# Deferred vector operations, a one-engine state chain, earlier bias loads and an unsplit modulation in a hybrid decoder step

## Chip, cores and metric

The kernel runs on one NeuronCore of a Trainium2 chip. The metric is the device time of one execution in microseconds (us); before the change it is 2248.98 us, the median of three runs (2247.84 to 2250.97). Engines are called as in the profile: PE (matrix multiply; PEld is its weight load), DVE (vector), ACT (scalar, with the activation functions), POOL (GpSimd) and SP, which issues the DMAs. All five run their own instructions in program order and wait for each other on semaphores.

## The reference

One layer of a conditioned decoder, for a prompt of 2048 tokens and eight sampled sequences of four tokens, model width 1024. The part of the reference that matters:

```
mod = silu(c) @ w_ada + b_ada                       # c: 1 + 8 rows of 1024; w_ada 1024 x 3072
shift, scale, gate = split(mod, 3)
h = rms(x, norm_g) * (1 + scale) + shift
proj = h @ w_in + b_in                              # 1024 x 7176, split into nine parts
y_h = head_rms(hgrn2(q, log f, v), hgrn_norm_g) * silu(hz)              # 8 heads of 128
y_m = (head_rms(sigmoid(mo) * mlstm(...), mnorm_g) + skip * xc) * silu(mz)   # 4 heads of 256
out = x + gate * (concat(y_h, y_m) @ w_out);  y = rms(out, final_g)
```

Both recurrences are computed chunk by chunk, with the state carried from chunk to chunk. All arithmetic is fp32.

## The kernel before

**Precision.** A plain fp32 matrix multiply is slow on PE, so the large products are split: an operand is written as a rounded part (type fp32r, made by ACT) and a remainder (made by DVE or POOL), and three products of parts are summed. `split` (line 205) does this for weights.

**Staging.** The prompt is cut in four segments of 512 tokens (`SEG`), a segment in four chunks of 128. First the modulation is computed (`ada_rows`, line 451): sixteen pieces of w_ada of 512 KB each are loaded, split by ACT and by DVE or POOL (line 461), and multiplied with `scs`, the split silu(c), into four PSUM tiles; `ada_shift_scale` (line 471) adds their two halves, transposes them and adds b_ada and 1. Then `x_modulate` (line 400) writes the normalized, modulated input as `hhi` and `hlo`. After that come 48 units per segment (`run_unit`, line 1444), one per 128 or 256 columns of w_in. A narrow unit is 24 matmuls of 512 columns in two steps (`proj_ct`, line 543), a wide one ("v" and "mo") 24 matmuls of 256 columns for each of four chunks (`proj_tok`, line 556). Split weights are written to DRAM in segment 0 and read back in segments 1 to 3. Last comes the output projection (line 1743).

**Order of the work.** The order on every engine is the order in which the program emits it. Next to the unit streams a list `rec` of generators: one per HGRN head (`hgrn`, line 601), one per mLSTM head (`mlstm`, line 1093), one for the convolution (`conv`, line 1008), and some others. After each step of a unit, `pump` (line 576) first issues stores that have come due, and then lets every generator in `rec`, oldest first, emit its next step. A generator that is appended later stands later in the list. Weights run ahead through a ring of four 8 KB slots per partition (`w8`) and a ring of three raw tiles. PSUM is a ring of eight tiles (`ps_tile`, line 123), taken in turn.

**Chains that the change touches.** A sigmoid is three ACT operations (line 94). In `hgrn` the decays are a sigmoid and a logarithm on ACT, then a scan, a copy and a subtraction on DVE (lines 612 to 616) and a scaling on POOL (617); two steps later, two exponentials, and the products `Ep` and `tn` (630, 631), which PE reads three steps on (639). The state chain of a head (lines 669 to 680) goes chunk by chunk: DVE adds (`U`, 677), POOL scales (678). `hgrn_out` scales by the norm (859) and gates (873, 877), and reads PSUM in both. `mlstm_out` (1291) takes the norm of a head by four ACT squares, a logarithm and an exponential, has DVE make `kap` of it (1313) and POOL scale `num` with it (1315); PE transposes `num` three steps later (1324), and DVE finishes the head (1333 to 1338). `head` and `c_split` (1104, 1127) prepare a chunk of the mLSTM. `bd_prep` (1533) builds block-diagonal weights in segment 0. `bias_bc` (1370) loads the bias of a "v" or "mo" unit at its start. `x_next` (1666) loads an input tile of the next segment and scales it at once on POOL.

Of the kernel before, what the change touches and what calls it, by code (L numbers as in the profile page):

```python
# [8 lines left out]
F32 = mybir.dt.float32  # L9
# [8 lines left out]
P = 128  # L18
# [49 lines left out]
def hymba_step(ctx, tc, flag, halved, x_prompt, x_sample, c_prompt, c_sample, state_hgrn, state_C, state_n, state_m,  # L68
# [140 lines left out]
    class Unit:  # L209
# [26 lines left out]
        def split(self, j):  # L236
# [4 lines left out]
            split(self.raw.pop(j), self.hi[:, :, c], self.lo[:, :, c], pool if self.src is w_in else vec)  # L241
# [7 lines left out]

    def C(nm, k):  # L250
        return cols[:, col[nm] + k:col[nm] + k + 1]
# [4 lines left out]
    sct = S2("sct", [P, KD, 1 + NSEQ])  # L256
# [4 lines left out]
    vec.tensor_tensor(sct[:, :, 1:], sgc[:, KD:].rearrange("p (s k) -> p k s", k=KD),  # L261
                      acol[:, 32:96].rearrange("p (s k) -> p k s", k=KD), op=ALU.mult)

    ML = 32 + 1 + NSEQ + 1
    scs = con.tile([P, KD, ML], F32R, name="scs")
    scp = S2("scp", [P, KD, ML])
    vec.memset(scp, 0.0)
    vec.tensor_copy(scs, scp)
    vec.tensor_copy(scs[:, :, :1 + NSEQ], sct)
    vec.tensor_tensor(scs[:, :, 32:33 + NSEQ], sct, scs[:, :, :1 + NSEQ].bitcast(F32), op=ALU.subtract)  # L270
# [172 lines left out]
    NB = 1 + NSEQ  # L443

    def ada_piece(n):
        k, b = divmod(n, 2)
        t = Bt("wada", [P, D]) if n % 2 else raw_tile()
        sync.dma_start(t, w_ada[k * P:k * P + P, b * D:b * D + D])
        return t

    def ada_rows(step):

        acc = [ps_tile("pada") if b % 2 else ps_tile("pada") for b in range(4)]
        raw = {n: ada_piece(n) for n in range(4)}
        for n in range(2 * KD):
            k, b = divmod(n, 2)
            step(n)
            r = raw.pop(n)
            t = ring.tile([P, 2, D], F32R, tag="w8", name="wadas", bufs=4)
            act(t[:, 0], r, AF.Copy)  # L460
            (pool if n % 4 == 3 else vec).tensor_tensor(t[:, 1], r, t[:, 0].bitcast(F32), op=ALU.subtract)
            for g in range(2):
                c = slice(512 * g, 512 * g + 512)
                for y in range(2):
                    pe.matmul(acc[2 * b + g][:ML], scs[:, k], t[:, y, c], start=(k == 0 and y == 0),
                              stop=(k == KD - 1 and y == 1))
            if n + 4 < 2 * KD:
                raw[n + 4] = ada_piece(n + 4)
        return acc

    def ada_shift_scale(acc):
        rows = Bt("arows", [NB, D])
        rows2 = Bt("arows", [NB, D])
        for b in range(4):
            dst = (rows, rows2)[b // 2][:, 512 * (b % 2):512 * (b % 2) + 512]
            act(dst, acc[b][:NB], AF.Copy)
            vec.tensor_tensor(dst, dst, acc[b][32:32 + NB], op=ALU.add)
        for r, dst, one in ((rows, msh, 0.0), (rows2, msc, 1.0)):
            ps = ps_tile("padt")
            for k in range(KD):  # L480
                pe.transpose(ps[:, k * NB:k * NB + NB], r[:, k * P:k * P + P], ident[:NB, :NB])
            v = ps[:, :KD * NB].rearrange("p (k b) -> p k b", k=KD)
            c0 = KD if one else 0
            vec.scalar_tensor_tensor(dst, v, one, acol[:, c0:c0 + KD, None].to_broadcast([P, KD, NB]),
                                     op0=ALU.add, op1=ALU.add)
        vec.tensor_tensor(msc, msc, C8("norm_g")[:, :, None].to_broadcast([P, KD, NB]), op=ALU.mult)
# [87 lines left out]
    stores = deque()  # L574

    def pump(n=1):
        for _ in range(n):
# [6 lines left out]
            for g in list(rec):  # L584
                if next(g, "end") == "end":
                    rec.remove(g)

# [13 lines left out]
    def hgrn(s, h, d):  # L601
# [10 lines left out]
        vec.tensor_tensor_scan(G[:, :W], hmask[:, :W], G[:, :W], 0.0, op0=ALU.mult, op1=ALU.add)  # L612
        g4 = G[:, :SEG].rearrange("p (c u t) -> p c u t", u=2, t=CH // 2)
        mid = small("mid", [P, NCH, 1])
        vec.tensor_copy(mid, g4[:, :, 0, CH // 2 - 1:CH // 2])
        vec.tensor_tensor(g4[:, :, 0], g4[:, :, 0], mid.to_broadcast([P, NCH, CH // 2]), op=ALU.subtract)
        pool.tensor_scalar(tn[:, :W], tn[:, :W], noml[:, h:h + 1], oml[:, h:h + 1], op0=ALU.mult, op1=ALU.add)  # L617
# [11 lines left out]
        vec.tensor_tensor(beta[:, :NCH - 1], sm[:, 0:NCH - 1], sm[:, NCH + 1:2 * NCH], op=ALU.mult)  # L629
        vec.tensor_tensor(Ep[:, :W], hq[:, :W], Ep[:, :W], op=ALU.mult)  # L630
        vec.tensor_tensor(tn[:, :W], tn[:, :W], G[:, :W], op=ALU.mult)
# [37 lines left out]
        for c in range(NCH):  # L669
# [180 lines left out]
    def hgrn_out(s, h, po, ops):  # L850
# [4 lines left out]
        for c in range(NCH):  # L855
# [3 lines left out]
        vec.tensor_tensor(on[:, :SEG].rearrange("p (c v) -> p c v", c=NCH), po.rearrange("p (c v) -> p c v", c=NCH),  # L859
                          f[:, :, None].to_broadcast([P, NCH, CH]), op=ALU.mult)  # L860
# [12 lines left out]
        vec.tensor_tensor(sz[:, :W], sz[:, :W], y[:, :W], op=ALU.mult)  # L873
# [3 lines left out]
        vec.scalar_tensor_tensor(y[:, :SEG], pn, C("hg", h), sz[:, :SEG], op0=ALU.mult, op1=ALU.mult)  # L877
        if smp:
            pn = ps_tile("pn")
            pe.matmul(pn[:, :NSM], onesm, sq)  # L880
            act(sq, pn[:, :NSM], AF.Ln, bias=epsc)
            act(sq, sq, AF.Exp, scale=-0.5)
            vec.scalar_tensor_tensor(ops, ops, C("hg", h), sq, op0=ALU.mult, op1=ALU.mult)
            vec.tensor_tensor(y[:, SEG:], ops, sz[:, SEG:], op=ALU.mult)
        y_store(s, h, y, W)
# [122 lines left out]
    def conv(s, i, j, d):  # L1008
# [28 lines left out]
        vec.tensor_tensor(xc[:, :W], xc[:, :W], e[:, :W], op=ALU.mult)  # L1037
# [55 lines left out]
    def mlstm(s, i, d):  # L1093
# [10 lines left out]
        def head(c):  # L1104
# [6 lines left out]
            vec.tensor_tensor(dm[:, t], ps[:, :CH], dm[:, t], op=ALU.mult)  # L1111
            st = small("st", [P, 2, CH], 2, F32R)
            act(st[:, 0], dm[:, t], AF.Copy)
            vec.tensor_tensor(st[:, 1], dm[:, t], st[:, 0].bitcast(F32), op=ALU.subtract)
            xw = small("xw", [P, 2, 2 * P], 1, F32R)
            wc = zc[:, c, 2, i:i + 1]
            act(xw[:, 0], ps[:, CH:CH + 2 * P], AF.Copy, scale=wc)
            vec.scalar_tensor_tensor(xw[:, 1], ps[:, CH:CH + 2 * P], wc, xw[:, 0].bitcast(F32), op0=ALU.mult,
                                     op1=ALU.subtract)
            if first and c == 0:  # L1120
                return st, xw, None
# [3 lines left out]
            return st, xw, qs  # L1125

        def c_split():
            t = small("Ch", [P, 2, 2, DH + 2], 1, F32R)
            act(t[:, 0], Cc, AF.Copy)
            vec.tensor_tensor(t[:, 1], Cc, t[:, 0].bitcast(F32), op=ALU.subtract)  # L1130
            return t
# [6 lines left out]
        ch = None if first else c_split()  # L1138
        yield
        yield  # L1140
        for c in range(NCH):
            st, xw, qs = cur
# [25 lines left out]
            if c + 1 < NCH:  # L1168
                ch = c_split()
# [121 lines left out]
    def mlstm_out(s, i, d, num, nums):  # L1291
# [7 lines left out]
        for nm, n, nch, og, floor in sets:  # L1299
# [19 lines left out]
        for j in range(2):  # L1319
# [13 lines left out]
            vec.tensor_tensor(szm[:, j, :W], szm[:, j, :W], e[:, :W], op=ALU.mult)  # L1333
# [538 lines left out]
```

## Time and profile before

| | |
|---|---|
| median of three runs | 2248.98 us |
| the profiled execution | 2243.03 us, its span 2241.2 us |
| instructions | 35168 |
| mean granted clock of PE in it | 0.989 of full |
| data moved by DMA | 405.26 MB, 181 GB/s over the span |

The profiled execution is 1.8 us longer than its span, and 5.95 us (0.3%) shorter than the median of the runs. The busy time of PE is not all work at its peak, since the ends of matmuls are modelled; what an engine's idle time was ended by is inferred from semaphores. A plain fp32 matmul leaves two records of PE in the trace, one of a split product leaves one.

### The profile page before, as it was taken

To read this page: it belongs to the slowest core of one execution; us is meant where nothing else is said; L and a number is where in the kernel's file an instruction comes from. 1 tells how busy PE (TensorE), PEld (TensorE's weight loads), DVE (VectorE), ACT (ScalarE), POOL (GpSimd) and SP (SyncE) were. 2 spreads that over 40 slices of the span, in tenths; PEclk is the share of its full clock that TensorE was granted. 3 is DMA by queue.
4 is the path that set the end of the run, shared out by engine and by line. 5 is a ranking of instruction groups with operands and counts; after the bars stand their busy time and mean duration, and the time that the engine had idled before them with its cause. 6 is when DMAs were issued, how large, how long until landed. Compare 5 with 4: busy or idle time off the path is not lost.

```text
span 2241.2 us, 35168 instructions
## 1 busy us (share of the span) xinstructions
PE 2170.0 (97%) x13594; PEld 1915.1 (85%) x13594; DVE 1268.8 (57%) x2664; ACT 979.1 (44%) x2260; POOL 432.0 (19%) x436
## 2 busy tenths in 40 slices
PE   6999999999999999999999999999999998999998
PEld 3888998787899889899988898888899987888885
DVE  7675657566756574566574555655455675423232
ACT  6445554464443354353444454534444535212121
POOL 3424353341112020212010212110101033000000
PEclk8999999999999999999999999999999999999999
DMA  7676766864546465634465555454555566533330
GB/s 257 214 234 219 262 221 205 302 227 155 189 152 228 167 230 193 217 136 158 179 203 202 189 192 180 162 169 163 146 194 161 174 193 173 165 108 96 93 99 27
DMA packets 225318, 405.26 MB, mean 181 GB/s; under 512 B 24843, under 2 KB 168627, under 8 KB 196470
## 3 DMA queue, kind: packets, MB, share of 16 engines
q1 hardware_dynamic: 225142, 402.92, 54.2%
q8 instruction: 109, 1.79, 0.3%
q14 instruction: 67, 0.55, 0.1%
HBM read 298.43 MB, written 104.44 MB: 180 GB/s over the span
## 4 chain that ended last, share of the span: by engine, by line
PE 68%; DVE 4%; ACT 3%; DMA 1%; issue 1%; POOL 1%; SPq 0%; DVEq 0%; ACTq 0%; POOLq 0%
PE pct L549 27%; PE pout L1743 15%; PE ptok L563 11%; PE p L1151 1%; PE pc L1135 1%; PE pv L1064 1%; PE pp L663 1%; PE pa L639 1%; PE pq L1081 1%; PE po L687 1%; PE po L689 1%; PE psx L1108 1%; ACT st L92 1%; PE p L1135 1%; DMA raw<-in_w_out_dram 1%
## 5 line engine op out<-in xcount | busy, mean ns | idle before, releaser
L549 PE MATMUL pct<-hhi,w 128*128 128x512 f32 (+1 forms) x3200 | 852.0, 354 | 1.2 <-DVE S L697 1.2
L549 PEld LDWEIGHTS pct<-hhi,w 128*128 128x128 f32 x3200 | 552.9, 188 | 74.4 <-issue 3.3
L549 PE MATMUL pct<-hlo,w 128*128 128x512 f32 (+1 forms) x1600 | 560.6, 350 | 0.0
L549 PEld LDWEIGHTS pct<-hlo,w 128*128 128x128 f32 x1600 | 301.0, 188 | 39.2
L563 PE MATMUL ptok<-whi,hhi 128*128 128x256 f32 x1024 | 301.4, 294 | 4.4 <-ACT hhi L92 3.3
L563 PE MATMUL ptok<-whi,hlo 128*128 128x256 f32 x1024 | 291.2, 284 | 0.2 <-DVE hlo L426 0.2
L563 PE MATMUL ptok<-wlo,hhi 128*128 128x256 f32 x1024 | 290.9, 284 | 0.0
L1743 PE MATMUL pout<-wh,y 128*128 128x512 f32 (+1 forms) x792 | 247.2, 391 | 3.0 <-ACT wh L92 3.0
L563 PEld LDWEIGHTS ptok<-whi,hhi 128*128 128x128 f32 x1024 | 197.4, 193 | 7.8 <-ACT hhi L92 3.7
L563 PEld LDWEIGHTS ptok<-wlo,hhi 128*128 128x128 f32 x1024 | 197.6, 193 | 2.3 <-issue 2.2
L563 PEld LDWEIGHTS ptok<-whi,hlo 128*128 128x128 f32 x1024 | 197.3, 193 | 0.9 <-DVE hlo L426 0.9
L1743 PEld LDWEIGHTS pout<-wh,y 128*128 128x128 f32 (+1 forms) x792 | 148.2, 187 | 35.8 <-ACT wh L92 3.5
L1743 PE MATMUL pout<-wl,y 128*128 128x512 f32 (+1 forms) x408 | 159.8, 392 | 1.1 <-POOL wl L1780 0.6
L92 ACT ACTIVATE xo<-oo 128x512 f32<-128x512 f32 (+1 forms) x34 | 21.5, 632 | 249.5 <-DVE oo L1831 249.5
L92 ACT ACTIVATE e<-e 128x512 f32<-128x512 f32 (+1 forms) x160 | 102.0, 638 | 58.9 <-DVE e L1034 54.8
L1826 DVE TENSOR_TENSOR oo<-pout,gate 128x512 f32<-128x512 f32 x32 | 22.0, 687 | 186.3 <-PE pout L1743 185.4
L617 POOL TENSOR_SCALAR tn<-tn,noml,oml 128x512 f32<-128x512 f32 (+1 forms) x32 | 52.6, 1643 | 385.5 <-ACT G L92 384.8
L207 POOL TENSOR_TENSOR w<-raw,w 128x1024 fp32r<-128x1024 f32 x40 | 97.2, 2436 | 113.5 <-ACT w L92 95.1
L121 POOL TENSOR_SCALAR num<-num,fin 128x256 f32<-128x256 f32 x64 | 35.1, 566 | 401.7 <-DVE fin L1313 357.8
L1161 DVE SCALAR_TENSOR_TENSOR Cc<-Cc,dec,pc 128x258 f32<-128x258 f32 x120 | 52.4, 478 | 84.0 <-PE pc L1135 84.0
L1743 PEld LDWEIGHTS pout<-wl,y 128*128 128x128 f32 (+1 forms) x408 | 75.6, 185 | 19.7 <-POOL wl L1780 1.3
L1032 DVE SCALAR_TENSOR_TENSOR xc<-mu,cols,xc 128x512 f32<-128x512 f32 (+1 forms) x120 | 83.7, 698 | 4.2
(403 smaller groups left out, 3792.2 us busy)
## 6 DMA issues: line engine op xcount, KB each, us to landing
w<-wdr SPq DMA_DIRECT2D x120, 1024.0 KB
wdr<-w SPq DMA_DIRECT2D x40, 1024.0 KB
raw<-in_w_in_dram SPq DMA_DIRECT2D x56, 512.0 KB
whi<-wdr SPq DMA_DIRECT2D x24, 1024.0 KB
wlo<-wdr SPq DMA_DIRECT2D x24, 1024.0 KB
raw<-ydr SPq DMA_DIRECT2D x29, 512.0 KB
xt<-in_x_prompt_dram SPq DMA_DIRECT2D x28, 512.0 KB
raw<-in_w_ada_dram SPq DMA_DIRECT2D x16, 512.0 KB
```

The lines of the kernel that those rows point to most:

```text
L92: nc.scalar.activation(out, in_, func, bias=bias, scale=scale, **kw)
L121: pool.tensor_scalar(out, in_, sc, 0.0, op0=ALU.mult, op1=ALU.add)
L207: eng.tensor_tensor(lo, raw, hi.bitcast(F32), op=ALU.subtract)
L549: pe.matmul(ps[:, :n], w[:, k, :], h[:, k, t0:t0 + n], start=(i == 0), stop=(i == 3 * KD - 1))
L563: pe.matmul(ps[:, :2 * P], h[:, k, t0:t0 + n], w[:, k, :], start=(i == 0), stop=(i == 3 * KD - 1))
L617: pool.tensor_scalar(tn[:, :W], tn[:, :W], noml[:, h:h + 1], oml[:, h:h + 1], op0=ALU.mult, op1=ALU.add)
L639: pe.matmul(pa[:, t], kt[:, t], qt[:, t])
L663: pe.matmul(pp[:, c * CH:c * CH + CH], ktT[:, c], v[:, c, vc])
L1032: vec.scalar_tensor_tensor(o, src(r), C("cw", 8 * r + k), o, op0=ALU.mult, op1=ALU.add)
L1135: pe.matmul(out[:, :DH + 2], a[:, x], b[y][:, c], start=(q == 0), stop=(q == 2))
L1161: vec.scalar_tensor_tensor(Cc[:, j], Cc[:, j], dec[:, i, c:c + 1], pcs[j][:, :DH + 2], op0=ALU.mult, op1=ALU.add)
L1743: pe.matmul(acc[g][:n if n == CH else 2 * n], a, b[:, 512 * g:512 * g + 512], start=(k == 0 and q == 0), stop=(k == KO - 1 and q == len(mm ...
```

## The change

**Deferred operations.** A queue `late` is added. DVE operations that need the result of an ACT chain of their own step are put into it instead of being emitted in place, and `pump` emits all of them, in the order in which they were put in, after the last generator of the step. This concerns `hgrn` (scan, copy, subtraction and POOL's scaling; and `beta`, `Ep`, `tn`), `hgrn_out` (line 859; and 873 to 885 with the store), `conv` (1037), and `mlstm_out` (1313 to 1315; and 1333 to 1339 with the store).

**State chain.** The scaling of line 678 goes from POOL to DVE (`R[0]` at 668 stays on POOL). **mLSTM head.** `c_split` becomes a part of `head`, and the order there becomes: ACT `xw`, DVE `dm`, ACT `Ch` and `st`, DVE `xw`, `Ch`, `st`. **Block-diagonal weights.** `bd_fill` in `bd_prep` (24 of them) goes from DVE to POOL. **Bias and x.** The bias of the next "v" or "mo" unit is loaded at the end of the one before it; a tile of x is scaled a unit, or in the last unit of a segment half a step, later than it is loaded.

**Modulation.** w_ada comes in eight loads of 1 MB into the `w8` ring and is not split; `sct` (silu(c), padded to 32 columns) is the stationary operand of plain fp32 matmuls, four for each load, which write four groups of 32 partitions of one PSUM tile. One copy, four transposes, two additions and a multiplication follow. The vectors' loads go four at a time, and the weights of the first unit are split by ACT and DVE instead of ACT and POOL.

```diff
+    sct = S2("sct", [P, KD, 32])
+    pool.memset(sct, 0.0)
...
+    def ada_load(k):
+        t = ring.tile([P, 2 * D], F32, tag="w8", name="wada", bufs=4)
+        sync.dma_start(t, w_ada[k * P:k * P + P, :2 * D])
...
+        acc = ps_tile("pada")
+        w = {k: ada_load(k) for k in range(4)}
+        for k in range(KD):
+            step(k)
+            t = w.pop(k)
+            for q in range(4):
+                pe.matmul(acc[32 * q:32 * q + 32], sct[:, k], t[:, 512 * q:512 * q + 512], start=(k == 0),
+                          stop=(k == KD - 1), skip_group_check=True)
+            if k + 4 < KD:
+                w[k + 4] = ada_load(k + 4)
...
     def ada_shift_scale(acc):
+        r = Bt("arows", [P, 512])
+        vec.tensor_copy(r, acc)
+        ps = ps_tile("padt")
+        for c in range(4):
+            pe.transpose(ps[:, c * P:c * P + P], r[:, c * P:c * P + P], ident)
...
             for g in list(rec):
                 if next(g, "end") == "end":
                     rec.remove(g)
+            while late:
+                late.popleft()()
...
-                pscale(nxt, u, sc)
+                vec.tensor_scalar(nxt, u, sc, None, op0=ALU.mult)
...
-        vec.tensor_tensor(xc[:, :W], xc[:, :W], e[:, :W], op=ALU.mult)
+        late.append(lambda: vec.tensor_tensor(xc[:, :W], xc[:, :W], e[:, :W], op=ALU.mult))
...
-            vec.tensor_tensor(kap, ss, rh, op=ALU.mult)
-            for c in range(nch):
-                pscale(nm[:n, c, :DH], nm[:n, c, :DH], f[:n, 3, c:c + 1])
+            def scale(nm=nm, n=n, nch=nch, f=f):
+                vec.tensor_tensor(f[:n, 3, :nch], f[:n, 2, :nch], f[:n, 1, :nch], op=ALU.mult)
+                for c in range(nch):
+                    pscale(nm[:n, c, :DH], nm[:n, c, :DH], f[:n, 3, c:c + 1])
+            late.append(scale)
...
-            bb = bias_bc((OI if kind == "v" else OMO) + 2 * n * P)
+            bb = bias.pop(u)
...
+        if kind in ("v", "mo"):
+            bias_load(u + 1)
...
-                bd_fill(bo[:, (k - 2) % 4, 0], 2, k - 2, vec)
+                bd_fill(bo[:, (k - 2) % 4, 0], 2, k - 2, pool)
...
+    def ada_step(k):
+        if k < 4:
+            for d in row_loads[4 * k:4 * k + 4]:
+                sync.dma_start(*d)
+        if k == 0:
+            x0.append(x_load(0, 1))
+        if k in (2, 4):
+            x_norm(k // 2 - 1)
+        if k == 3:
+            gate_prep()
+        if k == 4:
+            pre.extend(x_transpose(x0[0][0], CH, g) for g in range(2))
+        if k == 5:
+            cols_prep()
+    x0.append(x_load(0, 0))
     acc = ada_rows(ada_step)
...
     ada_shift_scale(acc)
-    stream_unit(0)
+    stream_unit(0, vec)
```

## Rows read from the trace of the kernel before

**Rows 1.** The busy time of each engine over the whole span, from the profile's page: us, share of the span, instructions.

```profile
PE 2170.0 (97%) x13594; PEld 1915.1 (85%) x13594; DVE 1268.8 (57%) x2664; ACT 979.1 (44%) x2260; POOL 432.0 (19%) x436
```

**Rows 2.** Stretches of the span: the stretch and its length, busy us of each engine with its instructions, granted clock of PE as a share of full, busy share of the DMA engines, GB/s.

```profile
0.00:47.00 47.00, 26.06 (x101) 12.41 (x101) 35.62 (x70) 28.66 (x45) 18.07 (x14) 0.91 0.76 270
47.00:500.00 453.00, 435.45 (x2832) 388.27 (x2833) 294.90 (x624) 238.00 (x528) 185.54 (x122) 0.98 0.71 233
500.00:1500.00 1000.00, 990.52 (x6630) 895.66 (x6629) 601.93 (x1327) 467.73 (x1137) 157.74 (x218) 1.00 0.53 185
1500.00:1900.00 400.00, 387.55 (x2582) 349.31 (x2581) 230.35 (x510) 181.23 (x416) 68.29 (x81) 0.99 0.54 169
1900.00:2241.20 341.20, 330.45 (x1456) 269.48 (x1455) 106.00 (x136) 63.50 (x136) 2.40 (x1) 0.99 0.34 100
```

**Rows 3.** The same view for two short stretches in which the granted clock fell.

```profile
118.00:130.00 12.00, 7.85 (x40) 7.01 (x39) 10.51 (x31) 4.56 (x17) 1.11 (x3) 0.72 0.58 208
1545.00:1556.00 11.00, 7.58 (x23) 5.69 (x24) 6.01 (x13) 6.50 (x16) 3.60 (x6) 0.69 0.17 54
```

**Rows 4.** What PE waited for, over the whole span: waiting tile and line, engine and line it waited for, us in total, times, longest.

```profile
PE ph L1324 <- POOL num L121: 6.7, 4, 4.2
PE po L689 <- DVE R L674: 4.2, 3, 3.2
PE pb L1542 <- DVE bt L1554: 4.2, 1, 4.2
PE pa L639 <- DVE tn L631: 3.6, 5, 1.1
```

**Rows 5.** The timeline from the last piece of w_ada to the first projection, rows of several engines: start, us, engine, line, operation, tiles, count, and the idle time before with what ended it.

```profile
31.03 1.06 ACT L92 ACTIVATE wadas<-wada 128x1024 fp32r<-128x1024 f32 x1 [0.25 <-DMA wada<-in_w_ada_dram]
35.51 1.21 DVE L461 TENSOR_TENSOR wadas<-raw,wadas 128x1024 fp32r<-128x1024 f32 x1
39.70 1.03 PE L397 MATMUL pxt<-ident,xt 128*128 128x128 f32 x8
41.42 0.23 DVE L484 SCALAR_TENSOR_TENSOR msh<-padt,acol 128x72 f32<-128x72 f32 x1
44.01 1.37 DVE L411 TENSOR_SCALAR hst<-pxt,msc,msh 128x128 f32<-128x128 f32 x4
45.45 1.16 ACT L92 ACTIVATE hhi<-hst 128x512 fp32r<-128x512 f32 x2
46.15 0.58 PE L563 MATMUL ptok<-whi,hhi 128*128 128x256 f32 x1 [3.27 <-ACT hhi L92]
```

**Rows 6.** Stretches of the start (columns as in Rows 2).

```profile
4.00:24.00 20.00, 10.53 (x33) 3.95 (x32) 14.74 (x28) 13.25 (x25) 7.26 (x4) 1.00 1.02 398
24.00:28.00 4.00, 2.98 (x7) 1.30 (x8) 3.57 (x3) 3.91 (x5) 1.34 (x2) 0.66 0.65 206
```

**Rows 7.** Plain fp32 matmuls. The first two are of PE's timeline: eight products of 128 columns into groups of 32 partitions (line 706), and the matmul after them. The others are of the groups by line, shapes apart (busy us and mean ns of one; then idle before) and of the instructions on tile `pada` and `arows` (duration ns min/median/max, first and last start).

```profile
319.86 0.65 PE L706 MATMUL pqs<-S,Ep 128*32 128x128 f32 x16
320.44 0.52 PE L549 MATMUL pct<-hhi,w 128*128 128x272 f32 x2
...
L1081 PE MATMUL pq<-xc,bm 128*128 128x512 f32 x48 | 22.6, 592 | 0.0
...
L477 DVE TENSOR_TENSOR arows<-arows,pada x4: 671/676/679, 38.7 to 40.7; 9x512 f32<-9x512 f32 x4
```

**Rows 8.** What DVE waited for, over the whole span (columns as in Rows 4).

```profile
DVE fin L1313 <- ACT fin L92: 55.1, 20, 3.1
DVE U L677 <- POOL R L121: 48.7, 89, 2.6
DVE v L1486 <- DMA bb<-in_b_in_dram: 28.9, 9, 5.4
DVE mo L1486 <- DMA bb<-in_b_in_dram: 17.0, 4, 7.7
```

**Rows 9.** The state chain's pieces (instructions on tile `R`), a fill on POOL (tile `bdf`) and on DVE (tile `bt`), and one row each of the timelines of DVE and POOL at 111 us.

```profile
L677 DVE TENSOR_TENSOR U<-R,pp x120: 275/287/290, 124.8 to 1839.2; 128x128 f32<-128x128 f32 x120
L121 POOL TENSOR_SCALAR R<-U,beta x88: 365/372/374, 125.2 to 1838.7; 128x128 f32<-128x128 f32 x88
...
L331 POOL TENSOR_TENSOR bdf<-bdw,oh x8: 388/487/844, 1481.9 to 1840.2; 128x128 f32<-128x128 f32 x8
...
110.78 2.39 DVE L933 COPY i<-gi 4x32 f32<-4x32 f32 x1
...
110.76 2.38 POOL L207 TENSOR_TENSOR w<-raw,w 128x1024 fp32r<-128x1024 f32 x1
```

**Rows 10.** Who waited for an instruction that writes `num` (us, times), and the wait of PE at 1548 us with what went before it on DVE.

```profile
  PEld ph L1324: 9.5, 10
  PE ph L1324: 6.7, 4
...
1547.56 0.16 DVE L1313 TENSOR_TENSOR fin<-fin 128x4 f32<-128x4 f32 x1 [3.13 <-ACT fin L92]
...
1548.42 2.69 PE L1324 MATMUL ph<-ident,num 128*128 128x128 f32 x8 [4.23 <-POOL num L121]
```

**Rows 11.** DVE's timeline ahead of PE's wait at 357 us.

```profile
351.05 0.72 DVE L1037 TENSOR_TENSOR xc<-xc,e 128x544 f32<-128x544 f32 x1 [2.71 <-ACT e L92]
351.69 0.49 DVE L1441 TENSOR_SCALAR szm<-pct,cols 128x272 f32<-128x272 f32 x1
```

More of the change, by code (lines that the diff above doesn't have):

```diff
@@ L234, in keep, with split @@
                     sync.dma_start(self.kept[i], x.bitcast(F32))
-        def split(self, j):
+        def split(self, j, eng):
             if self.again:
@@ L441, in toks @@
         return [(c, c * CH, CH) for c in range(NCH)] + ([(NCH, SEG, NSM)] if smp else [])
[L443 to L448, printed above, removed]
+    def ada_load(k):
+        t = ring.tile([P, 2 * D], F32, tag="w8", name="wada", bufs=4)
+        sync.dma_start(t, w_ada[k * P:k * P + P, :2 * D])
         return t
     def ada_rows(step):
[L453 to L468, printed above, removed]
@@ L473, in ada_shift_scale @@
[L473 to L485, printed above, removed]
+        r = Bt("arows", [P, 512])
@@ L574, in hymba_step @@
     stores = deque()
+    late = deque()
     def pump(n=1):
@@ L1117, in head @@
             act(xw[:, 0], ps[:, CH:CH + 2 * P], AF.Copy, scale=wc)
+            vec.tensor_tensor(dm[:, t], ps[:, :CH], dm[:, t], op=ALU.mult)
+            carry = not (first and c == 0)
+            ch = small("Ch", [P, 2, 2, DH + 2], 1, F32R) if carry else None
+            if carry:
+                act(ch[:, 0], Cc, AF.Copy)
+            st = small("st", [P, 2, CH], 2, F32R)
+            act(st[:, 0], dm[:, t], AF.Copy)
             vec.scalar_tensor_tensor(xw[:, 1], ps[:, CH:CH + 2 * P], wc, xw[:, 0].bitcast(F32), op0=ALU.mult,
                                      op1=ALU.subtract)
-            if first and c == 0:
-                return st, xw, None
+            if carry:
+                vec.tensor_tensor(ch[:, 1], Cc, ch[:, 0].bitcast(F32), op=ALU.subtract)
+            vec.tensor_tensor(st[:, 1], dm[:, t], st[:, 0].bitcast(F32), op=ALU.subtract)
+            if not carry:
+                return st, xw, None, None
             qs = small("qs", [P, 2, 2, CH], 2, F32R)
@@ L1368, in hymba_step, with bias_load @@
     start.append(len(units))
-    def bias_bc(c0):
-        t = small("bb", [P, 2 * P], 1)
-        sync.dma_start(t, bcast_ap(b_in[0, c0:c0 + 2 * P], P))
-        return t
+    bias = {}
+    def bias_load(u):
+        while u < len(units) and units[u][1] not in ("v", "mo"):
+            u += 1
+        if u < len(units):
+            c0 = (OI if units[u][1] == "v" else OMO) + 2 * units[u][2] * P
+            bias[u] = small("bb", [P, 2 * P], 1)
+            sync.dma_start(bias[u], bcast_ap(b_in[0, c0:c0 + 2 * P], P))
     KO = 2 * D // P
@@ L1391, in alloc, with split @@
             self.hi, self.lo = t[:, 0], t[:, 1]
-        def split(self, j):
-            split(self.raw, self.hi, self.lo)
+        def split(self, j, eng):
+            split(self.raw, self.hi, self.lo, eng)
     units += [(NSEG, "out", k, OutUnit(k)) for k in range(KA)]
@@ L1415, in stream @@
                 unit.alloc()
-            unit.split(j)
+            unit.split(j, eng)
             npiece[0] += 1
@@ L1585, in hymba_step @@
         x0.append(x_load(0, c))
-    pre = [x_transpose(x0[0][0], CH, g) for g in range(2)]
     ada_shift_scale(acc)
-    stream_unit(0)
+    stream_unit(0, vec)
     x_modulate(*x0[0], pss=pre, eng=None)
@@ L1674, in after_last @@
                 x_modulate(*nxt.pop(k_))
+            if k_ + 2 < NCH:
+                x_now(k_ + 2)
         for j in range(per):
@@ L1680, in hymba_step @@
                 x_next(1)
+            if j == per - 1 and not last:
+                x_now(0)
+                x_now(1)
             if j == (5 if s == 0 else 1 if last else 2):
```

117 lines of the change are left out of this document (57 added, 60 removed).

## The prediction

> **What bounds the kernel now.** I read the page's busy times first: PE is busy for 97% of the span, DVE for 57% [rows 1]. The reader should see that only two things can shorten this kernel: PE time in which PE waits, and PE time at the lower clock. Next come the stretches [rows 2]. The difference between a stretch and PE's busy time in it is what PE waited: 20.9 us in the first 47, 17.6 in 47 to 500, 9.5 in 500 to 1500, 12.5 in 1500 to 1900, and 10.8 behind that, where the change touches nothing. Then the granted clock: the two levels are 2.4 and 1.2 GHz, and 0.98 and 0.99 over 453 and 400 us stand for some 9 and 4 us lost by half clock. Two places show how this comes about [rows 3]: a wait of 4.2 us of PE for `num` lies in a stretch granted 0.69, so 0.31 * 11 = 3.4 us are lost behind the wait; the stretch at 118 us loses 0.28 * 12 = 3.4 us behind a wait of 4.2 us for `bt`. So a long wait costs nearly twice its length, and the whole steady part (47 to 1900 us) has 39.5 us of waits and some 13 us of lost clock to give. The waits of PE by releaser [rows 4] say who is late there: DVE (state chain, `bt`, `tn`) and POOL behind DVE (`num`). No transfer of projection weights is among them. The start is a separate problem with its own chain, read from the timeline [rows 5].
>
> **The start.** Now: ACT takes up the last piece of w_ada at 31.03, when it lands; splits by DVE and POOL trail behind it (DVE's last begins at 35.51), and the first projection matmul begins at 46.15 [rows 5], 15.1 us after the landing. New, step by step. Bytes ahead of the last landing: eight loads of 1.05 MB, two x tiles of 0.52 MB and the vectors, 9.5 MB. DMA moves 398 GB/s from 4 to 24 us, then falls to 206 because the next loads wait for buffers that the splits hold [rows 6]. In 20 us it has moved 7.96 MB; with four loads of 1 MB always ahead (10 us of transfer) the other 1.5 MB take 3.9 us, so the last load lands near 28, some 3 us earlier. PE: eight products of 128 columns into four column groups start 0.58 us before the next instruction, at full clock [rows 7], so four products of 512 columns take about 1.16 us, or 2.3 at half clock, where I expect this stretch; less than the 2.6 us in which a load lands. But `cols_prep` stands ahead of the sixth load's products and waits for the last vectors, which queue behind the seventh load, so two loads' products (4 us) end late and the last ends near 31. Then: a copy from PSUM (the nearest row has 0.68 [rows 7]), four transposes (eight took 1.03 [rows 5]; 0.6), two additions and a multiplication (0.23 each), 0.2 us of handover at four places: 33.5. DVE then makes both weight remainders (1.21 each at row L461) before `hst` (1.37), and ACT the first `hhi` (half of 1.16) [rows 5]: 33.5 + 2.4 + 1.4 + 0.6 = 37.9. **Gain 8.2 us**, as what follows (x tiles, units) keeps its distances. Bounds: landing no earlier than now gives 5; PE at full clock there gives 10.5.
>
> The Trainium skill, "DMA: Bandwidth & Descriptors", section "Where 436 GB/s comes from", has the HBM side of a core's transfers bind near 358 GB/s; the 398 above disagrees, and the measurement decides. By 358 the 9.5 MB would end 2.7 us later, an estimate from that page, and the gain at the start would be 5.5.
>
> **The steady part, edit by edit.** *Deferral* moves an operation only behind those of other generators in the same step. Where it already is the last of its step, nothing changes. That is the case ahead of PE's wait of 3.2 us for `R` [rows 4]: DVE waits 2.71 us for the convolution's sigmoid, and the row behind it is already the next step's PSUM read [rows 11]; a new HGRN head, too, is always last in the list, so its scan is. What can be filled are the waits of an older generator: `fin` (55.1 us in 20 waits) above all, whose generator stands ahead of the HGRN heads [rows 8]. I take half of it as filled, 25 us of DVE time. *State chain*: DVE waits 48.7 us for POOL's scalings [rows 8]; these go, and 120 scalings on DVE come. A PSUM-to-SBUF addition of this shape takes 0.287 [rows 9]; at 0.2 to 0.29 they are 24 to 35 us, so DVE gets 14 to 25 us, and a chain of three or four links gets shorter by its two handovers each. *Bias*: a "mo" unit's bias is now there ahead (17.0 us of DVE waits go); a "v" unit mostly follows a "mo" unit directly, so its load is issued at the same place as before and its 28.9 us mostly stay [rows 8]. The new load behind "v" makes SP wait for the last PSUM read of that unit; stores and weight loads stand behind it, but the weights wait for PE's end of the same unit anyway. I cost it at nothing; if the weights had no lead, it would cost one DVE operation a unit, 0.4 us * 16. *x scaling*: POOL and DVE are no longer held up by a tile still in flight; the tile's own landing is unchanged. *Fills*: 24 fills leave DVE and take 0.487 each on POOL [rows 9], 12 us in the first 170 us, beside weight splits. *mLSTM head*: the same operations in another order; between -3 and +3 us, I take 0.
>
> Together DVE gets some 70 of its waits back. That doesn't shorten the span by itself. Of the 39.5 us of PE waits about 25, and most of the lost clock, lie behind a late DVE; I take a quarter of 25 + 10, less 2 for new waits: **7 us**. Bounds: 20 (half of all and nothing new) and -5 (the fills' and deferrals' own delays).
>
> **Sum.** Against the profiled execution: 2243.0 - 8.2 - 7 = 2227.8. The median of the runs is 5.95 us above that execution, so in its terms 2249 - 15 = **2234**.
>
> **Rivals.**
> *A, waits only change places.* DVE is free earlier, but PE meets the next late producer. For it: the wait rows are spread over many tiles, none longer than 4.2 us [rows 4]. Only the start's 8.2 us remain: 2241.
> *B, the deferral makes `num` late (slower than before).* `kap` now comes after all other DVE work of its step, POOL's four scalings after it, and PE's transposes read that. In 10 of the 16 heads already the weight load waited for it, 9.5 us together, and PE itself 6.7 us in four [rows 10], so this chain has no slack there. DVE has 3.13 us to fill until ACT is done [rows 10]; if the other generators' work is longer than that by 2.5 us, the ten heads lose 25 us, plus clock: with four more stretches like those of [rows 3] some 8 us. 2249 - 8 + 25 to 33 = 2266 to 2274, if the other waits stay. It decides from 0.8 us a head on, where it eats the start's gain.
> *C, the scaling on DVE collides with POOL.* A copy of 4 x 32 elements took 2.39 us on DVE while POOL's split of 2.38 us ran [rows 9]. If DVE's new scalings (SBUF to SBUF, like that copy) are held up in the same way in segment 0, where splits run, 24 of them wait 1.2 us on average when they meet one; with all of them meeting one, 29 us of DVE's time go, and the steady gain with them: 2249 - 8 + 5 = 2246, within what counts as no change. The Trainium skill, "GPSIMD Engine Reference", section "Specifications", says that POOL shares its SBUF interfaces with DVE and contends with DVE instructions in a two-port mode or with two SBUF inputs; by that rule the trace's row is no accident. Against C: POOL's busy share is 19% [rows 1], and POOL's own scalings stood behind the same splits before.
> *D, the column groups don't overlap (the modulation doesn't do what it is meant to).* 48 records of unsplit 512-column products took 22.6 us [rows 7], 0.47 each; the 64 new ones would take 30 us at full and 60 at half clock instead of about 18. The start would end 7 to 37 us later than above: 2241 to 2271. Against it stands the row of line 706 [rows 7].
> *E, most DVE waits vanish*: 20 of the steady part and the start: 2220.
>
> **Chances.** Forecast 0.42, A 0.26, E 0.08, B 0.15, C 0.06, D 0.03. The likeliest is 2234. The range reaches from E's lower side (the sum of both upper bounds, 10.5 + 20, less what a run scatters) at 2216 up into B at 2260, which leaves out most of B and some of E. A measurement of this kernel can tell about 0.2%, 4.5 us, from no change. Faster than that: the forecast nearly whole, three quarters of A, E and a bit of D: 0.69. Within: a quarter of A, C: 0.13. Slower: B and most of D: 0.18.
>
> **What would show it.** The first projection matmul at 36 to 41 us, its products of one load within 2.5 us, and a DMA rate that doesn't fall before 27 us, show the start right. PE's waits between 47 (now about 39) and 1900 should sum to about 33, with no wait for POOL `R`, and none of DVE for "mo" biases. `pa`, `pb` and `po` should be shorter among PE's waits. If `ph` for `num` grows beyond 15 us, B is right; DVE scalings of 1 us and more in the first 500 us would be C. The prediction is wrong if the steady waits grow, or if they shrink by more than 20 us.

## The result and the profile after

The changed kernel took 2221.43 us (median of 4 runs, 2219.11 to 2222.18), the kernel before 2249.39 us (4 runs, 2247.84 to 2250.97): ratio 0.9874, 95% interval [0.9857, 0.9891], 28.0 us less. A second set of runs gave the same ratio (after_again below). The profiled execution of after took 2220.81 us, at its median; that of before took 2243.03 us, 3 to 6 us under its medians in all sets (2246.1 to 2249.4). So the two traces can account for 22.2 us of the 28; what the other executions of before do in the rest is in no trace here.

Busy time over the span of after, from the page; it answers [rows 1]:

```profile
PE 2157.2 (97%) x13582; PEld 1905.9 (86%) x13582; DVE 1268.1 (57%) x2746; ACT 957.6 (43%) x2240; POOL 382.9 (17%) x335
```

Stretches of after (columns as in rows 2): the five that answer to [rows 2], then two that answer to [rows 6] and one to [rows 3]:

```profile
0.00:38.00 38.00, 19.27 (x88) 6.32 (x88) 12.40 (x56) 10.64 (x25) 3.04 (x9) 0.75 0.94 338
38.00:500.00 462.00, 444.84 (x2915) 398.73 (x2915) 303.75 (x641) 241.91 (x539) 192.95 (x128) 0.98 0.71 235
500.00:1500.00 1000.00, 994.98 (x6689) 901.02 (x6689) 621.28 (x1403) 466.68 (x1138) 125.39 (x140) 1.00 0.53 185
1500.00:1880.00 380.00, 369.73 (x2448) 331.82 (x2447) 225.85 (x513) 174.93 (x406) 59.08 (x57) 1.00 0.56 173
1880.00:2219.00 339.00, 328.41 (x1448) 268.06 (x1446) 104.86 (x135) 63.42 (x136) 2.39 (x1) 0.99 0.34 99
...
4.00:24.00 20.00, 10.84 (x52) 2.75 (x52) 3.81 (x22) 4.34 (x15) 2.24 (x2) 0.83 1.02 407
24.00:28.00 4.00, 2.88 (x17) 0.30 (x16) 0.29 (x1) 0.00 (x0) 0.00 (x0) 0.74 1.02 392
...
1528.00:1539.00 11.00, 7.84 (x30) 6.10 (x31) 5.92 (x13) 6.16 (x15) 3.19 (x6) 0.84 0.17 54
```

Take PE's busy time from each stretch: between the start and the output part PE now waits 17.2 + 5.0 + 10.3 = 32.5 us, where it was 39.5 us. PE's busy time behind the start fell from 2144.0 to 2138.0 us for the same matmuls. About half of that is clock, by an estimate: the mean granted clock of the whole span (0.989 before, 0.988 after) less that of the start (0.92 up to the first projection matmul before, 0.76 after) leaves some 21 us lost to the lower clock behind the start before and some 18 after. The rest of the 6.0 us is not traced. The wait for `num` near 1531 us now stands in a stretch granted 0.84 instead of 0.69. The DMA rate no longer falls between 24 and 28 us.

The start of after, timeline rows that answer to [rows 5] (start, us, engine, line, operation, count, idle before):

```profile
28.38 1.94 PE L460 MATMUL pada<-wada,sct 128*32 128x512 f32 x8 [0.79 <-DMA wada<-in_w_ada_dram]
30.39 0.69 DVE L468 COPY arows<-pada 128x512 f32<-128x512 f32 x1 [6.00 <-PE pada L460]
32.93 2.36 DVE L207 TENSOR_TENSOR wlo<-raw,whi 128x1024 fp32r<-128x1024 f32 x2
35.21 1.36 DVE L415 TENSOR_SCALAR hst<-pxt,msc,msh 128x128 f32<-128x128 f32 x4
37.28 0.58 PE L554 MATMUL ptok<-whi,hhi 128*128 128x256 f32 x1 [3.27 <-ACT hhi L92]
```

Waits of PE and DVE in after (us in total, times, longest); they answer to [rows 4] and [rows 8]:

```profile
PE pb L1564 <- DVE bt L1576: 4.5, 1, 4.5
PE ph L1334 <- POOL num L121: 4.4, 3, 3.7
PE po L691 <- DVE R L676: 3.8, 2, 2.6
PE pa L641 <- DVE tn L631: 2.3, 3, 1.2
...
DVE fin L1321 <- ACT fin L92: 47.0, 20, 3.2
DVE v L1506 <- DMA bb<-in_b_in_dram: 24.5, 7, 5.2
DVE mo L1506 <- DMA bb<-in_b_in_dram: 5.2, 1, 5.2
```

So the 22.2 us by the traces are 8.9 at the start (first projection matmul 46.15 to 37.28), 7.0 of waits, 6.0 of PE's busy time, and 0.3 elsewhere. DVE's 48.7 us of waits for POOL's `R` are gone; of the wait for `fin` only 8.1 us went.

### The profile page after: what moved, and what is told of

Same layout as the page of the kernel before. It is cut to its first block, busy times and chain, and to the rows that moved or that the text cites. A ratio compares the mean times of both kernels' runs of the same rounds, so it can differ in the third digit from the quotient of the medians.

```text
span 2219.0 us, 35094 instructions
## 1 busy us (share of the span) xinstructions
PE 2157.2 (97%) x13582; PEld 1905.9 (86%) x13582; DVE 1268.1 (57%) x2746; ACT 957.6 (43%) x2240; POOL 382.9 (17%) x335
## 4 chain that ended last, share of the span: by engine, by line
PE 78%; DVE 8%; DMA 5%; ACT 4%; issue 3%; POOL 1%; SPq 0%; POOLq 0%; DVEq 0%; ACTq 0%
PE pct L540 30%; PE pout L1780 15%; PE ptok L554 14%; PE pc L1143 2%; PE p L1158 2%; PE pv L1072 1%; PE po L691 1%; PE po L689 1%; PE pq L1089 1%; DMA cs<-in_state_mlstm_C_dram 1%; PE psx L1116 1%; DMA wada<-in_w_ada_dram 1%; PE pa L641 1%; PE pp L665 1%; PE p L1143 1%
## 5 line engine op out<-in xcount | busy, mean ns | idle before, releaser
L92 ACT ACTIVATE e<-e 128x512 f32<-128x512 f32 (+1 forms) x160 | 102.1, 638 | 55.1 <-DVE e L1042 50.9
L92 ACT ACTIVATE num<-p,zc 128x257 f32<-128x257 f32 x60 | 28.3, 471 | 149.0 <-PE p L1158 149.0
```

What stands on the lines that cost most here:

```text
L92: nc.scalar.activation(out, in_, func, bias=bias, scale=scale, **kw)
```

## The experiments

Each ran in five rounds beside the kernel before. "First" is the start of the first projection matmul in the trace; runs of one set share the median of before. The three sets ran on different chips, so kernels of different sets are compared by their ratios; the intervals of the ratios are 0.1 to 0.2% to either side, 2 to 4 us.

| kernel | set | us | before | ratio [95%] | first |
|---|---|---|---|---|---|
| start_only | 1 | 2236.47 | 2246.80 | 0.9958 [0.9944, 0.9971] | 38.55 |
| defer_only | 1 | 2237.89 | 2246.80 | 0.9955 [0.9941, 0.9969] | 46.73 |
| chain_only | 1 | 2251.98 | 2246.80 | 1.0022 [1.0010, 1.0033] | 46.00 |
| loads_only | 1 | 2244.02 | 2246.80 | 0.9990 [0.9980, 0.9999] | 46.15 |
| after_again | 2 | 2219.76 | 2246.11 | 0.9874 [0.9858, 0.9891] | 37.15 |
| rest_only | 2 | 2236.75 | 2246.11 | 0.9955 [0.9942, 0.9969] | 45.93 |
| no_chain | 2 | 2219.75 | 2246.11 | 0.9877 [0.9862, 0.9892] | 37.88 |
| no_defer | 2 | 2235.80 | 2246.11 | 0.9955 [0.9941, 0.9968] | 37.00 |
| one_group | 3 | 2228.31 | 2247.85 | 0.9913 [0.9900, 0.9926] | 45.91 |
| head_only | 3 | 2237.20 | 2247.85 | 0.9954 [0.9942, 0.9966] | 46.17 |
| xs_now | 3 | 2223.39 | 2247.85 | 0.9896 [0.9882, 0.9910] | 37.99 |
| start_and_copies | 3 | 2220.74 | 2247.85 | 0.9876 [0.9861, 0.9890] | 39.29 |

**One part at a time.** The first four kernels are the kernel before with one part of the change.

start_only (the new `ada_rows`, `ada_shift_scale`, `ada_step`, first unit's split on DVE):

> Only the start is changed (unsplit modulation in column groups, order of its loads); the steady part is the kernel before. All theories: the first projection matmul at 37 to 38 us instead of 46.15. Theory P (the parts add up): the gain stays 9 us to the end, PE's waits between the first projection matmul and the output part stay at 39 to 40 us, ratio 0.996 (about 2240 us). Rival W (waits only change places, so any shift of the phase between the engines changes the clock falls too): the steady waits or the half-clock time change by over 4 us although no line of the steady part differs.

By the median it gains 10.3 us. Its first projection matmul stands at 38.55 us, 7.6 earlier, and its span is 6.6 us shorter. By the stretches its waits between 47 and 1900 us are 42.1 us, 2.6 more than in before, and the granted clock of these stretches is that of before (0.98, 1.00, 0.99): theory P, since rival W wanted over 4.

defer_only (`late`, and what is put into it):

```diff
+            while late:
+                late.popleft()()
```

> Only the deferral of DVE operations to the end of a step. The prediction had half of DVE's 55.1 us of waits for fin filled; the changed kernel still shows 47.0. Theory P: fin's wait falls to 45 to 50, PE's waits fall by 1 to 4 us, ratio 0.998 to 1.000. Rival D (deferral carries the steady gain): PE's waits fall by over 5 us, ratio under 0.997. Rival B of the prediction (deferral makes num late): ph's wait for num over 10 us, ratio over 1.002.

8.9 us less: rival D by the time, theory P by the waits, which are 38.0 us between 47 and 1900 us (39.5 before); those for `R` and `num` are 3.9 and 5.9 us, little less than in [rows 4]. Its span is only 4.1 us shorter; most of the other 4.8 us is the lead of 3.8 us that the profiled execution of before has over the median of this set.

chain_only:

```diff
-                pscale(nxt, u, sc)
+                vec.tensor_scalar(nxt, u, sc, None, op0=ALU.mult)
```

> Only the state chain's scaling on DVE instead of POOL. DVE's 48.7 us of waits for POOL's R go. Theory P (the chain is the largest part of the steady gain of 13 us): ratio 0.996 to 0.998, 4 to 8 us less, po's wait for R under 3 us, and the clock falls that lie behind late HGRN heads gone. Rival D: under 2 us, since those DVE waits lay beside PE's work. Rival C: DVE's scalings take 1 us and more beside POOL's splits in the first 500 us, and the time is that of before.

It is 5.2 us slower by the medians (10.8 by the spans of the two traces). Theory P fell; D, which allowed for a small gain, doesn't explain a loss, and C has the collision with POOL's splits but not the operations that it meets. Timelines of chain_only show what happens (POOL, DVE and PE at 223 to 229 us), and its clock there:

```profile
223.46 2.38 POOL L207 TENSOR_TENSOR w<-raw,w 128x1024 fp32r<-128x1024 f32 x1 [1.17 <-ACT w L92]
223.53 2.85 DVE L1338 TENSOR_TENSOR xs<-xs,szm 128x512 f32<-128x512 f32 x1
...
227.07 0.71 PE L687 MATMUL po<-v,atm 128*128 128x128 f32 x4 [1.54 <-DVE atm L644]
228.58 0.49 PE L689 MATMUL po<-R,Ep 128*128 128x128 f32 x2 [0.79 <-DVE R L674]
...
225.00:236.00 11.00, 8.67 (x42) 7.32 (x41) 9.87 (x21) 4.76 (x15) 0.84 (x1) 0.84 0.82 283
```

The same place in the kernel before:

```profile
222.06 0.69 DVE L1338 TENSOR_TENSOR xs<-xs,szm 128x512 f32<-128x512 f32 x1
...
225.32 0.37 POOL L121 TENSOR_SCALAR R<-U,beta 128x128 f32<-128x128 f32 x1 [4.51 <-DVE U L677]
227.23 2.39 POOL L207 TENSOR_TENSOR w<-raw,w 128x1024 fp32r<-128x1024 f32 x1
...
224.00:235.00 11.00, 10.40 (x61) 8.79 (x60) 8.94 (x16) 4.72 (x15) 3.47 (x4) 1.00 1.02 358
```

Read POOL first. In before its next weight split stands behind the scalings of `R` and starts at 227.23. With the scalings gone from POOL the split starts at 223.46, and DVE's multiplication of two SBUF tiles beside it takes 2.85 instead of 0.69 us. `atm` and `R[0]` stand behind that on DVE, so PE waits 1.54 and 0.79 us and the clock falls to 0.84. The scaling that was moved is not the one that is slowed (its median is 0.287 us, one of 88 takes 1.69): moving it let POOL run into other operations. A link of the chain got shorter by 0.15 us only (matmuls on `R` 0.79 us apart before, 0.64 here).

Set beside the same projection matmuls of before, those of chain_only fall back by 3.4 us between 214 and 235 us, by another 3.4 between 457 and 477, by 3.0 between 509 and 574, and no further behind that (times of before; POOL's last split in this part of chain_only starts at 488). The second of these is of the same kind: the split at 467.81 stretches `tn` to 2.88 us, and PE waits 2.79 us for `R`. The cause of the third stays open.

loads_only (`bias_load`, `x_now`):

> Only the bias loaded a unit ahead and the next segment's x loaded a unit ahead of its scaling. DVE's wait for mo biases falls from 17.0 to about 5, that for v biases from 28.9 to about 25. Theory P: DVE's wait for a bias rarely sets PE's, so 0 to 3 us, ratio 0.999 to 1.000; the clock fall at the segment change near 506 us goes or halves. Rival L (a bias that is waited for holds up DVE's whole queue, and the waits of PE for DVE come from there): over 5 us, ratio under 0.998.

2.8 us less, with an interval that nearly reaches zero: theory P. DVE's waits for biases fell to 4.4 ("mo") and 22.1 us ("v").

**The whole, and the whole without a part.**

> The changed kernel once more, beside the same runs of the kernel before as the three others of this set, so that each can be set against it. Both theories: ratio 0.986 to 0.989, 2215 to 2222 us.

As expected. rest_only (new order in the mLSTM head, fills on POOL):

> Only the reordered mLSTM head and the fills on POOL. The four parts run alone multiply to 0.9925, the whole has 0.9874, so some 11 us are missing. Theory Q (the parts add up, and the missing 11 us are in this part): ratio 0.994 to 0.996. Rival I (interaction: the chain's scalings on DVE pay only where deferral and the fills' move have freed DVE): ratio 0.998 to 1.001.

9.4 us less: theory Q. The ratios of the five parts multiply to 0.988, the whole has 0.9874, the same within the intervals.

no_chain (POOL scales `R` again, all else as after):

> The changed kernel with the state chain's scaling put back on POOL. Theory Q: the chain cost 5 us by itself and costs them here too, so this kernel is 4 to 6 us faster than the changed one (ratio to before 0.985). Rival I: it is 3 us or more slower than the changed kernel (ratio 0.989 or more).

Neither: the median of after_again (2219.75 and 2219.76), though DVE waits 48.1 us for POOL's `R` again. So the chain's place costs 5 us in the kernel before, and nothing that these runs can tell behind the other parts.

no_defer (all but `late`):

> The changed kernel without the deferral to the end of a step. Theory Q: deferral is worth 10 us here as by itself: ratio 0.991 to 0.993. Rival I: it is worth more than by itself, 14 us or more (ratio 0.994 or more), because the chain's scalings on DVE need the gaps that it fills. Third case: under 5 us, then the gain of the deferral alone was a shift of phase.

16.0 us more than after_again: rival I for the deferral. That is about what the deferral gains alone (8.9) and what the chain's place costs without it (5.2) together; a kernel without both was not run. PE's wait for `R` is back at the size that it has in chain_only (6.9 us, four times), and two clock falls are back. Of no_defer (PE's wait for `R`; its wait for `atm` at 217 us, with the DVE operation ahead of `atm`; two stretches):

```profile
PE po L680 <- DVE R L665: 6.7, 4, 2.9
...
214.31 2.89 DVE L1327 TENSOR_TENSOR xs<-xs,szm 128x512 f32<-128x512 f32 x1
217.88 0.71 PE L678 MATMUL po<-v,atm 128*128 128x128 f32 x4 [1.57 <-DVE atm L635]
...
214.00:225.00 11.00, 8.63 (x44) 7.46 (x43) 10.52 (x21) 3.19 (x14) 2.40 (x1) 0.84 0.67 221
460.00:471.00 11.00, 8.15 (x43) 7.36 (x42) 8.32 (x18) 2.94 (x12) 1.44 (x1) 0.84 0.77 260
```

Of after_again, the same two stretches and the timelines of POOL, DVE and PE ahead of the first:

```profile
214.00:225.00 11.00, 9.75 (x56) 8.27 (x55) 9.71 (x24) 4.72 (x15) 0.18 (x1) 1.00 0.88 302
460.00:471.00 11.00, 11.00 (x54) 9.21 (x53) 9.97 (x19) 6.29 (x11) 2.15 (x1) 1.00 0.83 298
...
208.96 2.42 POOL L207 TENSOR_TENSOR w<-raw,w 128x1024 fp32r<-128x1024 f32 x1 [0.86 <-ACT w L92]
211.76 2.42 POOL L207 TENSOR_TENSOR w<-raw,w 128x1024 fp32r<-128x1024 f32 x1 [0.38 <-ACT w L92]
...
208.95 0.74 DVE L646 COPY_PREDICATED atm<-causal,pa 128x512 f32<-128x512 int32 x1
209.59 0.73 DVE L1347 SCALAR_TENSOR_TENSOR xs<-ph,cols,xs 128x512 f32<-128x512 f32 x1
210.24 1.69 DVE L1349 TENSOR_TENSOR szm<-szm,e 128x512 f32<-128x512 f32 x1
211.96 2.77 DVE L1350 TENSOR_TENSOR xs<-xs,szm 128x512 f32<-128x512 f32 x1
...
216.33 0.49 PE L691 MATMUL po<-R,Ep 128*128 128x128 f32 x2 [1.25 <-DVE R L676]
```

The slowed multiplications are still there (1.69 and 2.77 us), but `atm`, which PE wants first, now stands ahead of them. Set beside the same projection matmuls of after_again, those of no_defer fall back by 2.6 us at this place and by 4.0 between 447 and 467 us (the second place of xs_now below); 11.2 us are lost by 575 us, and less than 1 from there to the output part. So two places hold 6.6 us; the rest of the 11.2 lies in the same early part of the span and was not traced to places.

**Inside the parts.** head_only is rest_only without the fills:

```diff
-            vec.tensor_tensor(dm[:, t], ps[:, :CH], dm[:, t], op=ALU.mult)
-            st = small("st", [P, 2, CH], 2, F32R)
-            act(st[:, 0], dm[:, t], AF.Copy)
...
             act(xw[:, 0], ps[:, CH:CH + 2 * P], AF.Copy, scale=wc)
+            vec.tensor_tensor(dm[:, t], ps[:, :CH], dm[:, t], op=ALU.mult)
```

> Only the mLSTM head's new order (the fills stay on DVE). Together with the fills it gave ratio 0.9955. The prediction gave the head 0 (between -3 and +3 us). Theory H (the head is what gained: PE's waits of 2.2 us for st and 0.8 for qs go, and many waits under 0.3 us with them): ratio 0.995 to 0.997, all of it between 160 and 1860 us. Rival F (the fills): 0.999 to 1.001, and the gain lay in the first 170 us.

10.6 us less: theory H; the fills add nothing that the intervals can tell (0.9955 with them, 0.9954 without). In before (waits of DVE, then the group of PE's matmuls on `Ch`: busy us, mean ns, idle before):

```profile
DVE st L1114 <- ACT st L92: 24.2, 64, 0.5
DVE Ch L1130 <- ACT Ch L92: 16.0, 39, 0.4
...
L1151 PE MATMUL p<-Ch,qs 128*128 128x258 f32 x360 | 54.7, 285 | 0.8 <-DVE qs L1124 0.6
```

The same in head_only:

```profile
DVE dm L1114 <- ACT xw L92: 21.9, 41, 3.6
...
L1150 PE MATMUL p<-Ch,qs 128*128 128x258 f32 x360 | 52.9, 282 | 0.0
```

DVE did `dm`, waited for ACT's half of `st` in each of 64 head parts, and later for its half of `Ch` in 39 of them; the waits are short, 0.4 us each. In the new order ACT has `xw` to do while DVE makes `dm`; 40.2 us of such waits go and 21.9 come; DVE's wait for PE at the next link of the chain (`Cc`) grows from 84.0 to 97.9 us, so DVE gets there earlier. PE's group is shorter by 1.8 us and its idle time by 0.8; its group on `st` by 0.7 and 0.7. The trace's span is 6.8 us shorter: it first falls 2 us back (by 131 us) and gains between 430 and 1560 us. So the run shows that the order gains, and PE's two groups show 4.0 us of it; that the rest comes by the same waits is argued, not shown.

xs_now (one deferral undone):

```diff
-            late.append(finish)
+            finish()
```

> The changed kernel with one of its deferrals undone, that of the mLSTM unit's end (the two multiplications that write xs, and szm), which in the first 500 us meet POOL's weight splits and then take 2.8 us each instead of 0.7. Theory X (deferral pays by putting what PE waits for, the masked atm and the state chain, ahead of such stretched operations): PE's waits for po at 216 us and near 470 us come back (2.3 us each, a clock fall of 3.4 us behind each), 4 to 10 us slower than the changed kernel, ratio to before 0.989 to 0.992. Rival Y (deferral pays by filling DVE's waits for ACT, fin above all, wherever they are): within 2 us of the changed kernel, since this is one of seven deferrals and none of fin's.

By medians 3.6 us more than after_again and 2.0 more than after; by the ratios to before (0.9896 and 0.9874) 0.22%, 4.9 us: theory X at its lower end, and Y not excluded by the medians alone. Its trace shows why only half came: at 216 us `atm` stands behind the stretched multiplications again, but PE waits only 0.80 us twice, 1.60 where after_again has 1.25, without a clock fall; at 458 us the wait is back and the clock falls. DVE's last operations ahead of `R`, PE's wait and the clock there, and `R` in after_again:

```profile
456.21 0.71 DVE L1349 TENSOR_TENSOR szm<-szm,e 128x544 f32<-128x544 f32 x1
456.96 0.72 DVE L1350 TENSOR_TENSOR xs<-xs,szm 128x544 f32<-128x544 f32 x1
457.60 0.35 DVE L676 TENSOR_SCALAR R<-pp,beta 128x128 f32<-128x128 f32 x1
...
458.00 0.49 PE L691 MATMUL po<-R,Ep 128*128 128x128 f32 x2 [2.42 <-DVE R L676]
...
455.00:466.00 11.00, 8.59 (x43) 7.63 (x42) 8.61 (x20) 2.94 (x12) 0.00 (x0) 0.84 0.68 235
```

```profile
456.24 0.33 DVE L676 TENSOR_SCALAR R<-pp,beta 128x128 f32<-128x128 f32 x1
```

At this place theory X has the wrong reason. The operations of the unit's end that stand ahead of `R` are not stretched here (0.71 and 0.72 us, and 0.89 for the addition at 455.40); in after_again PE doesn't wait, because `R` stands ahead of them, although `tn` before it is stretched to 2.88 us. The wait is the length of work that PE doesn't need, put first.

one_group:

```diff
-                pe.matmul(acc[32 * q:32 * q + 32], sct[:, k], t[:, 512 * q:512 * q + 512], ...
+                pe.matmul(acc[q][:32], sct[:, k], t[:, 512 * q:512 * q + 512], ...
```

> The changed kernel, but the four products of a w_ada load go to four PSUM banks at partitions 0 to 31 (one column group) instead of four groups of one bank, and four copies of 32 partitions replace the one of 128. The arithmetic is the same. Theory O (the four groups run at the same time): the products of one load take 1.9 us and more at full clock and 3.5 to 4 us at half clock instead of 1.07 to 1.94, the first projection matmul comes at 40 to 44 us instead of 37.3, ratio to the changed kernel 1.001 to 1.003. Rival D (they never overlapped): products as before, only the copies' 1.5 us are added, first projection matmul at 38.8.

Theory O, and more than it asked: one load's products take 3.62 us in one group and 1.06 in after, both at a granted clock of 1.00 (1.94 in after where it is 0.50), and the first projection matmul stands at 45.91, as in before. (The edit also spreads the products over four banks; no run separates that from the groups.) One row of one_group and one of after:

```profile
25.15 3.62 PE L460 MATMUL pada<-wada,sct 128*32 128x512 f32 x8
```

```profile
23.99 1.06 PE L460 MATMUL pada<-wada,sct 128*32 128x512 f32 x8
```

start_and_copies, the one try at a better kernel:

```diff
-                vec.tensor_copy(t[:, 2:4], ps[:, :2 * P].rearrange("p (a b) -> p a b", a=2))
+                act(t[:, 2:4], ps[:, :2 * P].rearrange("p (a b) -> p a b", a=2), AF.Copy)
...
         if k == 4:
+            load_pieces(1)
+            x0.append(x_load(0, 1))
```

> The changed kernel with two more edits. First: the 16 copies of the block-diagonal preparation on ACT instead of DVE; ACT stands idle for 8.9 us before 108.6 where DVE is 4.4 us late with bt. If ACT is free there, PE's wait of 4.45 us for bt at 113 us and the clock fall of 3.4 us behind it go. Second: x tile 1 and the first two weight pieces change places behind the w_ada loads, and DVE makes hst between the two weight remainders instead of behind both. If the last load's landing and DVE's order set the start, the first projection matmul comes at 34 to 35 us instead of 37.3. Both: 8 to 11 us less than the changed kernel, 2209 to 2213 us. Rival: other waits take their place (ACT late with Ep or hhi), and the time stays within 3 us of the changed kernel.

The rival, at both places:

```profile
33.28 1.15 ACT L92 ACTIVATE hhi<-hst 128x512 fp32r<-128x512 f32 x2
37.67 1.97 PE L406 MATMUL pxt<-ident,xt 128*128 128x128 f32 x8 [6.74 <-POOL xt L121]
...
114.24 0.80 PE L699 MATMUL po<-R,Ep 128*128 128x128 f32 x2 [3.70 <-DVE R L684]
```

`hhi` starts 3.3 us earlier, but the transposes of x tile 1 stand ahead of the first projection on PE and wait 6.74 us for the tile that was put back; the first projection starts at 39.29. At 113 us the wait of 4.45 us for `bt` is gone, and one of 3.70 us for `R` stands in its place.

## Why the prediction was right, and where it was not

The forecast was 15 us less, the measurement 28, inside the range. That it lies inside owes something to luck: the range was 44 us wide, the start was understood, and the terms of the steady part were mostly not. By its own steps:

*The start* was sized well: 8.2 forecast, 8.9 in the trace, 10.3 in the run of that part alone. The last load's products began at 28.38, when it landed (forecast near 28), and ended at 30.3 (near 31); the first projection began at 37.28 (37.9); one load's products took 1.06 to 1.94 us (1.16 to 2.3). The wait that was feared from `cols_prep` came at the sixth load, as forecast (1.50 us at 23.76), but the two loads behind it were still waited for (0.72 us at 25.78, 0.79 at 28.38), so it held nothing up. The terms listed from the last product to `msc` add up to 33.8 and not 33.5, which changes little. One_group shows that the column groups carry the gain: without them the unsplit products alone bring nothing. Rival D was priced at 7 us and more for the same arithmetic; 8.6 were measured, so it was the condition that failed, not the price. The Trainium skill, "TensorE: Matmul & The Clock Gate", section "Part 3: Packing small matmuls — row/col tiling", gives 2.38 times for three column groups. Here four groups gave 3.62 / 1.06 = 3.4 times, which goes the same way. The Trainium skill, "DMA: Bandwidth & Descriptors", section "Where 436 GB/s comes from", has the HBM side of a core's transfers bind near 358 GB/s, half of what a stack gives to two cores. The trace passes that after the change too: 407 GB/s from 4 to 24 us, with one core at work.

*The steady part* is the step that failed: 7 us forecast, 13.3 in the traces, about 18 by medians (28 less 10). Its sign for PE's waits came true (32.5 us, forecast about 33), as did those for POOL's `R` and for `num`; but it took the waits and the lost clock together as 7 us, and PE's busy time gave 6.0 more. PE's longest wait for `bt` did not shrink (4.2 to 4.5), and one wait for a "mo" bias is left (5.2). Of the terms by edit three were wrong, and they partly cancelled. The mLSTM head was taken at 0 (between -3 and +3) and is worth 10.6 alone: the prediction counted the same operations and not the order in which DVE and ACT hand them to each other. The state chain was counted as a gain, from DVE's 48.7 us of waits; alone it costs 5.2, and with the rest it is worth 0. The deferral was argued from half of `fin`'s 55.1 us; only 8.1 us of that wait went, but it is worth 8.9 us alone and 16.0 in the whole. At two places the traces show how: it puts `atm` ahead of multiplications that POOL's splits stretch (216 us, where undoing the unit's end alone gives only 0.35 us of wait back), and `R` ahead of the unit's end, which PE doesn't need (458 us). The rest of its gain was not traced to places; alone, only 4.1 of its 8.9 us are in a trace. The bias and x loads brought 2.8, about what their waits allowed, and the fills nothing that can be told.

*Rival C* named the right mechanism for the wrong victim: the moved scalings run at 0.287 us, while the multiplications of `xs`, `szm` and `tn` meet the splits. *Rival B* did not come: PE's wait for `num` fell from 6.7 to 4.4 us. (Its price was also too low by its own rows: four stretches of 3.4 us are 13.6 us of lost clock, not 8.) *Rival E* gave the right time (2220) by a way that didn't happen. *Rival A* was true of single places, as start_and_copies shows, but not of the whole. The reading that a long wait costs nearly twice its length held at `bt` after the change (4.45 us, then 0.25 * 12 = 3.0 of lost clock from 112 to 124 us) and not at `num` (3.7 us, then 0.16 * 11 = 1.8). What stays open is the 6 us by which the medians' difference exceeds that of the traces.

## What to carry to other kernels

A wait of an engine that isn't the bottleneck is worth what stands behind it, not its length: taking away 48.7 us of DVE waits gained nothing or cost 5 us, and a new order that took away 18 of 40 us of short ones, in a chain of two engines that PE follows, gained 10. An operation that is taken off an engine lets that engine's next work start earlier: ask what that will meet before the time is counted as won. Where two engines slow each other, order can hide what can't be avoided: put what PE waits for ahead of what gets stretched, and ahead of whatever PE doesn't wait for.

## What the runs showed of the hardware

A DVE multiplication of two SBUF tiles of 512 columns took 0.69 us alone (222.06 in before) and 2.85 beside a POOL split of 2.38 (223.53 in chain_only), ending 0.5 us behind it; two operations with an input in PSUM took 0.74 and 0.73 beside one (208.95 and 209.59 in after_again). The Trainium skill, "GPSIMD Engine Reference", section "Specifications", has POOL and DVE share their SBUF interfaces and contend when DVE is in a two-port mode or has two SBUF inputs. The multiplications agree; the copy of [rows 9] has a single input and was held up as well, and no run shows in which mode it was. Four fp32 products in four column groups took 1.06 us where one group took 3.62, both at a granted clock of 1.00. In the first 38 us PE was busy for 19.27 us and granted 0.75 of its clock in after; in one_group it was busy for 29.60 us and granted 1.00.
